# Half B's tap sums wait for half A's norm buffers; the second and third weights are split ahead of the second token block; edge factors are made later

## The chip, the core and the metric

The kernel runs on one core of a Trainium2 chip. TensorE (PE) multiplies matrices, VectorE (DVE), ScalarE (ACT) and GpSimd (POOL) work element by element, SyncE (SP) issues the DMA transfers, and each engine executes its own list of instructions strictly in the order in which it was built; semaphores hold an instruction until what it reads is there. The metric is the device time of one execution, in microseconds (us).

## What is computed

A decoder trunk of two layers over 2048 tokens of 1024 channels, in float32. In outline, with the parts that the change touches kept:

```python
h = rmsnorm(x, even_norm)
proj = h @ even_w_in                       # pool 512 | ssm 512 | gate 1024
u_pool, u_ssm, z = proj[..., :512], proj[..., 512:1024], proj[..., 1024:]
pooled = windowed_mean(u_pool, (2, 4, 8, 16)) - u_pool   # divided by min(pos, window)
y = concat(pooled @ pool_w * pool_scale, s5(u_ssm)) * silu(z)
x = x + y @ even_w_out

h = rmsnorm(x, odd_norm)
val, gt, z = split(h @ odd_w_in, 3)
c = causal_depthwise_conv(val * sigmoid(gt), conv_w) + conv_b      # 31 taps
c = layernorm(c) * ln_g + ln_b                                     # over the channels
x = x + (silu(c) * silu(z)) @ odd_w_out
out = rmsnorm(x, final_norm)
```

## The kernel before

The tokens are cut into two halves, A and B, of 1024 tokens, and each half into two blocks of 512. Every weight and every activation is split into a high part, rounded to the fast float32 format, and a low part, the rest; a product is three matmuls (high by high, high by low, low by high). ACT makes the high part and DVE the low one by a subtraction.

The PE's list is a row of units: for half A the layer-0 projections `A.s0` to `A.s3` (inputs of the state-space part), `A.pu`, `A.pz`, `A.z`, then the same for B; then `A.glu`, `A.o`, the layer-1 projections of A, `B.glu`, `B.o`, those of B, and at the end `A.q` and `B.q`, the two output projections. The first three units run block by block: `A.s0.0`, `A.s1.0`, `A.s2.0` on the first token block, then `A.s0.1` and so on. A unit's sums stand in one of three PSUM buffers `mm` until another engine has taken them out, so the fourth unit can't begin before the first is emptied. `B.q` ends with four units on B's second token block.

Nothing of the order is written out by hand. While the kernel is built, `Sched` runs all the work as threads (`gen`, `conv_load`, `ln_thread`, `x_rates` and others), each of which yields one operation at a time, or waits for a key (`Wait`, `done`), or for a free buffer (`Alloc`). From all threads' next operations it takes the one that can start first on its engine by its own clock; among those of one engine that could start within `SLACK` of it, the thread with the smallest priority number goes first. Its clock uses a duration for each operation (`tt`, `ts`, `mmb` and others) and adds a margin `PAD` after the producer. The chip sees only the lists that result: these numbers decide which instruction stands where, and no time in them is a time on the chip.

Four pieces of work matter below.

- **Weights.** `fetch_thread` loads them, `split_thread` makes the two parts. The first job has priority 0, the others have `RANK["split"]`, which is 2; the activations (`x_split`) have 1.
- **Token rates.** `x_rates` computes the reciprocal root mean square of each token: ACT squares, then for half A six small POOL instructions, a PE transposition of an 8 by 128 tile (`aux<-ident,sml`), an ACT copy, and a trip through the DRAM buffer `rsd` that spreads the rates over the partitions (`st<-rsd`). `post_u` needs them before it can empty a unit's `mm` (`po<-mm,st`).
- **State-space tables.** `ssm_tables` (DVE), `ssm_w` and `ssm_g` prepare four groups of tables, many small DMAs among them; `ssm_g` transposes a group's table in two lots on the PE (`aux<-ident,act`, four each) and ACT copies them out of the two `aux` buffers.
- **Tap sums and the norm.** `conv_thread` adds the 31 taps of a channel tile on DVE, in two accumulators from the pool `ca`, which has four tiles. Three of half B's eight channel tiles are summed on the PE instead (`pe_conv`). `ln_thread` normalizes one token block of one half over the channels: it loads four tiles, sums them, takes the mean with a PE product against `onesN` (`aux<-st,onesN`), squares on ACT, and applies the rate. Half A's two blocks (A0, A1) and B's second (B1) take their four tiles from `ca`, B's first (B0) from `act`; so A1 can load only when all four `ca` tiles are free. B0 and B1 start when half A's activations for `A.q` are all there.

`setup` makes `corr`, sixteen factors for each pooling window that correct the first tokens; `pool_thread` uses them.

Of the kernel before, what the change touches and what calls it, by code (L numbers as in the profile page):

```python
# [34 lines left out]
GATE_R = 'A.pz1'  # L35
GATE_S = 'B.s0.1'
SLACK = {"PE": 0.02, "V": 0.6, "A": 0.3, "G": 0.1, "SP": 0.3}
PAD = {("PE", True): 5.0, ("PE", False): 0.3, ("V", True): 1.0, ("V", False): 0.05, ("A", True): 1.0, ("A", False): 0.05}
SLOTS = dict(act=25, w=8, raw=2, st=8, po=2)
NSSM = 3  # L40
# [37 lines left out]
class Sched:  # L78
# [31 lines left out]
    def spawn(self, gen, prio, name=""):  # L110
        self.threads.append(Thread(gen, prio, name))
# [20 lines left out]
    def ready(self, op):  # L132
        r = 0.0
        for aps, wr in ((op.reads, False), (op.writes, True)):
            for ap in aps:
                nm, (lo, hi, p0, p1) = self.span(ap)
                dr = ap.space == bass.MemoryType.DRAM
                for (a, b, q0, q1), t, e, w in self.acc.get(nm, ()):
                    if dr and wr and w:
                        continue  # L140
                    if a < hi and lo < b and p0 < q1 and q0 < p1 and (wr or w) and not (e == op.eng == "PE"):
                        r = max(r, t + (PAD[op.eng, e == "SP"] if op.eng in "PE V A" else 0.05))
        return r

    def emit(self, op):
        start = max(self.clk[op.eng], op.ready)
# [102 lines left out]
def trunk(ctx, tc, io):  # L249
# [43 lines left out]
    def width(o):  # L293
        return int(np.prod(o.shape[1:]))
# [19 lines left out]

    def tt(o, a, b, op, eng=None):
        if eng is G:
            d = 1.0 + 0.2 * width(o) if op == ALU.pow else 0.6 + width(o) * 2e-3
            return Op("G", d, [a, b], [o], lambda: G.tensor_tensor(o, a, b, op))  # L318
        d = vdur(0.16, 1.035e-3, o, a, b)
        return Op("V", d, [a, b], [o], lambda: V.tensor_tensor(o, a, b, op))  # L320

    def ts(o, a, s1, s2=None, op0=ALU.mult, op1=None, eng=None):
        rd = [a] + [s for s in (s1, s2) if isinstance(s, bass.AP)]
        e = eng or V

        def emit():
            if op1 is None:
                e.tensor_scalar(o, a, s1, None, op0)  # L328
            else:
                e.tensor_scalar(o, a, s1, s2, op0, op1)  # L330
        if eng is G:
            return Op("G", 0.6 + width(o) * 1e-3, rd, [o], emit)
        return Op("V", 0.165 + width(o) * (1.03e-3 if isps(a) else 0.55e-3), rd, [o], emit)

    def stt(o, a, s, b, op0, op1):
# [171 lines left out]
    jobs = []  # L507
# [167 lines left out]
    def x_load(h, b, acts, gate=None, job=None):  # L675


        if gate:
            yield Wait(gate)
        if job:  # L680
            job.raw = yield Alloc("raw")
        for kp in range(4):
            yield from acts.alloc(kp, b)
            xt = yield Alloc("st")
            if job:
                r = jobs_parts[job][kp]
                yield dma(job.raw[:, r], job.src[:, r])
                done("raw", job, kp)
            yield dma(xt[:, :1024], io["xT"][h, b, kp])
            spawn(x_split(h, xt, acts, kp, b), 1, f"xs{h}{b}{kp}")  # L690
            done("x", h, b, kp)
# [787 lines left out]
    def conv_load():  # L1479
        for h, j in conv_order:  # L1480
            yield Wait(("g", h, j))
            gt = yield Alloc("cg")
            if h == 0:
                yield gset(gt[:, :HL], 0.0)
            else:
                yield dma(gt[:, :HL], gd[0][j][:, H - HL:H])
            yield dma(gt[:, HL:HL + H], gd[h][j])
            cgt[h, j] = gt
            yield Wait(("cw",))
            ca, cb = cas[h, j] = yield Alloc("ca", 2)  # L1490
            yield act(ca[:, :H], gt[:, 0:H], AF.Identity, bias=vc("conv_b", j), scale=cwt[:, j, 0:1])
            yield act(cb[:, :H], gt[:, 1:H + 1], AF.Copy, scale=cwt[:, j, 1:2])
            done("cg", h, j)
# [145 lines left out]
    def ln_thread(h, b, out, gate=None):  # L1639
# [5 lines left out]
        pool = "act" if h == 1 and b == 0 else "ca"  # L1645
        pools = (pool,) * 4
        ct = yield Alloc(pool, 4)
        cc = [c[:, :1024] for c in ct]
        for kp in range(4):
            yield dma(k2(cc[kp]), cd[h][kp][:, :, bs])  # L1650
# [197 lines left out]
    def setup():  # L1848
        yield act(junk[:, :16], mhalf, AF.Square)
        yield dma(vcol[:, :NV], io["vecs"])  # L1850
        done("vcol",)
        yield Wait(("x", 0, 1, 3))
        spawn(ssm_prep(), RANK["prep"], "prep")
        yield Wait(("boot", 3))
        for gi, w in enumerate(WINDOWS):
            yield ts(corr[:, gi, :], pos, float(w), 1.0 / w, ALU.min, ALU.mult)
        yield recip(corr, corr)
# [21 lines left out]
    jobs_parts[jobs[0]] = [slice(q * 256, q * 256 + 256) for q in range(4)]  # L1879
    spawn(main(), 4, "main")  # L1880
    spawn(setup(), 1, "setup")
    spawn(x_load(0, 0, h0[0], None, jobs[0]), 1, "x00")
    spawn(after(("x", 0, 0, 3), fetch_thread(jobs[1:])), 2, "fetch")
    spawn(split_thread(jobs[:1]), 0, "split0")
    spawn(after(("w", jobs[0]), split_thread(jobs[1:])), RANK["split"], "split")
    spawn(x_load(0, 1, h0[0], ("x", 0, 0, 3)), 2, "x01")
    spawn(x_rates(0, ("x", 0, 1, 3)), 3, "xr0")
    spawn(pool_fold(), 3, "fold")
# [73 lines left out]
```

## Time and profile before

| | |
|---|---|
| three runs | 1495.79, 1497.37, 1497.68 us; median 1497.37 |
| the profiled execution | 1496.72 us |
| its span, first to last instruction | 1494.9 us; 1.8 us lie around it |
| mean granted TensorE clock | 0.993 |
| busy: PE, DVE, ACT, POOL | 98%, 78%, 36%, 3% |

A row of the timeline gives start and duration in us, engine, line, operation, out<-in, shapes, how many, and in brackets the idle time of the engine before it with what ended it. A row of the waits gives engine, tile and line, what was waited for, and us in total, times, longest. A row of windows gives a stretch, the busy us of the engine asked for with its instructions, the granted TensorE clock, the share of DMA time and GB/s. A row of the chain gives start, us and what the end of the program hung on there.

### The profile page before, as it was taken

The page shows a single profiled execution, that of the slowest core. Times are in us where ns is not written, and L with a number is a line of the kernel's source. Part 1 is how long each engine was busy: PE and PEld are TensorE (multiplying, and loading weights), DVE is VectorE, ACT ScalarE, POOL GpSimd, SP SyncE. Part 2 cuts the span into 40 slices and gives each one's busy share as a digit, 9 for nine tenths or more (in the row PEclk, how much of TensorE's full clock was granted, in tenths as well). Part 3 has the DMA queues.
Part 4 walks back from the last instruction along what each step waited for, and adds up shares of the span by engine and source line. Part 5 has one row for each costly group of instructions (what it writes and reads, how often), then busy time and mean ns, then how long its engine had stood idle before and what let it go on. Part 6 is the DMA issues. An engine that isn't in the chain of part 4 may idle for free.

```text
span 1494.9 us, 17913 instructions
## 1 busy us (share of the span) xinstructions
PE 1460.0 (98%) x6672; PEld 1190.2 (80%) x6672; DVE 1159.5 (78%) x1435; ACT 545.2 (36%) x964; POOL 40.9 (3%) x103
## 2 busy tenths in 40 slices
PE   7898999999999999999999999999999999999997
PEld 5777888887788888888888888888888888878786
DVE  7987773999935124499999999996999997577852
ACT  6235331121143037212122431452235334446753
POOL 0100000000000001000000000100000000001000
PEclk9999999999999999999999999999999999999999
DMA  8579856677454456555655543646655468676853
GB/s 342 193 219 341 296 172 243 208 251 251 144 198 146 143 198 224 182 186 182 201 207 206 199 158 127 197 141 241 210 174 176 133 201 280 241 275 205 295 195 114
DMA packets 150311, 310.06 MB, mean 207 GB/s; under 512 B 38240, under 2 KB 60496, under 8 KB 150224
## 3 DMA queue, kind: packets, MB, share of 16 engines
q1 hardware_dynamic: 150224, 308.92, 60.7%
q8 instruction: 52, 0.85, 0.2%
q14 instruction: 35, 0.29, 0.1%
HBM read 192.18 MB, written 116.70 MB: 207 GB/s over the span
## 4 chain that ended last, share of the span: by engine, by line
PE 75%; DVE 11%; DMA 7%; SPq 2%; issue 2%; ACT 2%; POOL 0%; POOLq 0%; DVEq 0%; ACTq 0%
PE mm L402 70%; DVE st L320 4%; PE aux L402 3%; SPq L387 2%; DVE act L320 2%; DVE w L320 1%; DMA st<-x2d 1%; DVE st L348 1%; PE aux L416 1%; DMA y1d<-st 1%; DVE st L338 1%; DMA ca<-cd 1%; DMA st<-in_x 1%; DMA raw<-in_even_w_in 1%; DMA Md<-st 1%
## 5 line engine op out<-in xcount | busy, mean ns | idle before, releaser
L402 PE MATMUL mm<-act,w 128*128 128x512 f32 x4224 | 1002.6, 396 | 14.0 <-ACT act L364 6.4
L402 PEld LDWEIGHTS mm<-act,w 128*128 128x128 f32 x4224 | 792.1, 189 | 196.9 <-ACT act L364 6.9
L338 DVE SCALAR_TENSOR_TENSOR ca<-cg,cwt,ca 128x1024 f32<-128x1024 f32 (+1 forms) x435 | 463.3, 1136 | 4.3 <-ACT ca L364 4.3
L402 PE MATMUL mm<-w,act 128*128 128x512 f32 x1344 | 317.5, 396 | 1.1 <-DVE w L320 1.0
L402 PEld LDWEIGHTS mm<-w,act 128*128 128x128 f32 x1344 | 252.9, 189 | 60.3 <-DVE w L320 1.7
L320 DVE TENSOR_TENSOR w<-raw,w 128x1024 fp32r<-128x1024 f32 (+1 forms) x95 | 112.5, 1187 | 78.1 <-ACT w L352 76.6
L352 ACT CAST w<-raw 128x1024 fp32r<-128x1024 f32 (+1 forms) x95 | 96.6, 1017 | 118.9 <-PE mm L402 89.5
L364 ACT ACTIVATE junk<-st 128x1024 bf16<-128x1024 f32 (+1 forms) x64 | 54.0, 843 | 100.3 <-DVE st L320 81.2
L320 DVE TENSOR_TENSOR act<-st,act 128x512 fp32r<-128x512 f32 (+1 forms) x64 | 56.5, 922 | 25.9 <-ACT act L352 25.8
L364 ACT ACTIVATE po<-mm 128x1024 f32<-128x1024 f32 x28 | 28.8, 1028 | 126.0 <-PE mm L402 70.9
L364 ACT ACTIVATE st<-mm 128x1024 f32<-128x1024 f32 x24 | 24.7, 1027 | 130.6 <-PE mm L402 127.6
L352 ACT CAST act<-st 128x512 fp32r<-128x512 f32 (+1 forms) x64 | 52.0, 854 | 52.5 <-DVE st L338 15.6
L402 PE MATMUL aux<-st,act 128*128 128x64 f32 (+1 forms) x352 | 53.0, 293 | 1.4 <-DVE st L320 1.4
L320 DVE TENSOR_TENSOR st<-st,mm 128x512 f32<-128x512 f32 x48 | 31.0, 682 | 29.3 <-PE mm L402 29.0
L352 ACT COPY st<-aux 128x256 f32<-128x256 f32 (+3 forms) x46 | 18.0, 415 | 91.4 <-PE aux L402 78.6
L402 PEld LDWEIGHTS aux<-st,act 128*128 128x128 f32 x352 | 45.6, 191 | 6.0 <-DVE st L320 3.5
L318 POOL TENSOR_TENSOR sml<-sml,mhalf 128x1 f32<-128x1 f32 (+2 forms) x38 | 30.6, 817 | 650.4 <-DVE sml L328 355.4
L338 DVE SCALAR_TENSOR_TENSOR st<-st,mm 128x1024 f32<-128x1024 f32 x24 | 31.9, 1328 | 19.9 <-PE mm L402 13.1
L364 ACT ACTIVATE act<-act,mask 128x128 f32<-128x128 f32 x144 | 43.3, 390 | 8.7 <-DMA act<-band 8.7
L402 PE MATMUL mm<-act,act 128*128 128x512 f32 x192 | 45.1, 394 | 0.8 <-DVE st L320 0.8
L320 DVE TENSOR_TENSOR st<-st,act 128x512 f32<-128x512 f32 (+1 forms) x38 | 29.3, 772 | 20.9 <-DMA st<-x2d 14.9
L402 PEld LDWEIGHTS mm<-act,act 128*128 128x128 f32 x192 | 36.0, 188 | 9.5 <-DVE st L320 1.2
(148 smaller groups left out, 893.9 us busy)
## 6 DMA issues: line engine op xcount, KB each, us to landing
st<-x1d SPq DMA_DIRECT2D x48, 256.0 KB, 4.4
raw<-in_odd_w_in SPq DMA_DIRECT2D x24, 512.0 KB, 4.5
kept_h<-w SPq DMA_DIRECT2D x24, 512.0 KB, 3.0
kept_l<-w SPq DMA_DIRECT2D x24, 512.0 KB, 5.3
w<-kept_h SPq DMA_DIRECT2D x24, 512.0 KB, 3.7
w<-kept_l SPq DMA_DIRECT2D x24, 512.0 KB, 4.8
raw<-in_even_w_in SPq DMA_DIRECT2D x23, 512.0 KB, 5.4
st<-in_xT SPq DMA_DIRECT2D x16, 512.0 KB, 8.0
```

Of the source, the lines that this page charges most:

```text
L318: return Op("G", d, [a, b], [o], lambda: G.tensor_tensor(o, a, b, op))
L320: return Op("V", d, [a, b], [o], lambda: V.tensor_tensor(o, a, b, op))
L338: return Op("V", d, rd, [o], lambda: V.scalar_tensor_tensor(o, a, s, b, op0, op1))
L348: return Op("V", 0.2 + width(o) * 1.9e-3, rd, [o], lambda: V.tensor_tensor_scan(o, r.to_broadcast([128, width(o)]), x, ini, ALU.mult, ALU. ...
L352: return Op("A", adur(o, a, 0), [a], [o], lambda: A.copy(o, a))
L364: return Op("A", adur(o, a, n), rd, wr, lambda: A.activation(o, a, fn, **kw))
L387: lambda: SP.dma_start(out=o, in_=i))
L402: nc.tensor.matmul(o, w, x, start=s, stop=e)
L416: nc.tensor.transpose(o, a, idn)
```

## The change

Five edits. Half B's `conv_load` waits until A1 has its four `ca` tiles (`done("ln", h, b)` stands right behind that allocation). The second and third weights are split at priority 0, ahead of the activations of the second token block. The edge factors `corr` are made when `A.s3` begins, and not early in `setup`. The scheduler's margin for a PE operation that waits for a compute engine is 1.0 larger while its clock is below 200. Its durations for POOL operations are smaller. The last two change nothing but the order.

```diff
--- before.py
+++ after.py
@@ -35,6 +35,7 @@
 GATE_R = 'A.pz1'
 GATE_S = 'B.s0.1'
 SLACK = {"PE": 0.02, "V": 0.6, "A": 0.3, "G": 0.1, "SP": 0.3}
+EARLY, EARLY_END = 1.0, 200.0
 PAD = {("PE", True): 5.0, ("PE", False): 0.3, ("V", True): 1.0, ("V", False): 0.05, ("A", True): 1.0, ("A", False): 0.05}
 SLOTS = dict(act=25, w=8, raw=2, st=8, po=2)
 NSSM = 3
@@ -139,8 +140,15 @@
                     if dr and wr and w:
                         continue
                     if a < hi and lo < b and p0 < q1 and q0 < p1 and (wr or w) and not (e == op.eng == "PE"):
-                        r = max(r, t + (PAD[op.eng, e == "SP"] if op.eng in "PE V A" else 0.05))
+                        r = max(r, t + self.pad(op.eng, e == "SP", t))
         return r
+
+    def pad(self, eng, sp, t):
+
+        if eng not in "PE V A":
+            return 0.05
+        early = EARLY if t < EARLY_END and eng == "PE" and not sp else 0.0
+        return PAD[eng, sp] + early
 
     def emit(self, op):
         start = max(self.clk[op.eng], op.ready)
@@ -314,7 +322,7 @@
 
     def tt(o, a, b, op, eng=None):
         if eng is G:
-            d = 1.0 + 0.2 * width(o) if op == ALU.pow else 0.6 + width(o) * 2e-3
+            d = 0.35 + 0.2 * width(o) + 0.6 * (width(o) == 1) if op == ALU.pow else 0.19 + width(o) * 2e-3
             return Op("G", d, [a, b], [o], lambda: G.tensor_tensor(o, a, b, op))
         d = vdur(0.16, 1.035e-3, o, a, b)
         return Op("V", d, [a, b], [o], lambda: V.tensor_tensor(o, a, b, op))
@@ -329,7 +337,7 @@
             else:
                 e.tensor_scalar(o, a, s1, s2, op0, op1)
         if eng is G:
-            return Op("G", 0.6 + width(o) * 1e-3, rd, [o], emit)
+            return Op("G", 0.19 + width(o) * 1e-3, rd, [o], emit)
         return Op("V", 0.165 + width(o) * (1.03e-3 if isps(a) else 0.55e-3), rd, [o], emit)
 
     def stt(o, a, s, b, op0, op1):
@@ -1487,6 +1495,8 @@
             yield dma(gt[:, HL:HL + H], gd[h][j])
             cgt[h, j] = gt
             yield Wait(("cw",))
+            if h == 1:
+                yield Wait(("ln", 0, 1))
             ca, cb = cas[h, j] = yield Alloc("ca", 2)
             yield act(ca[:, :H], gt[:, 0:H], AF.Identity, bias=vc("conv_b", j), scale=cwt[:, j, 0:1])
             yield act(cb[:, :H], gt[:, 1:H + 1], AF.Copy, scale=cwt[:, j, 1:2])
@@ -1645,6 +1655,7 @@
         pool = "act" if h == 1 and b == 0 else "ca"
         pools = (pool,) * 4
         ct = yield Alloc(pool, 4)
+        done("ln", h, b)
         cc = [c[:, :1024] for c in ct]
         for kp in range(4):
             yield dma(k2(cc[kp]), cd[h][kp][:, :, bs])
@@ -1851,7 +1862,9 @@
         done("vcol",)
         yield Wait(("x", 0, 1, 3))
         spawn(ssm_prep(), RANK["prep"], "prep")
-        yield Wait(("boot", 3))
+
+    def pool_edges():
+        yield Wait(("u", "A.s3"))
         for gi, w in enumerate(WINDOWS):
             yield ts(corr[:, gi, :], pos, float(w), 1.0 / w, ALU.min, ALU.mult)
         yield recip(corr, corr)
@@ -1879,10 +1892,12 @@
     jobs_parts[jobs[0]] = [slice(q * 256, q * 256 + 256) for q in range(4)]
     spawn(main(), 4, "main")
     spawn(setup(), 1, "setup")
+    spawn(pool_edges(), 1, "edges")
     spawn(x_load(0, 0, h0[0], None, jobs[0]), 1, "x00")
     spawn(after(("x", 0, 0, 3), fetch_thread(jobs[1:])), 2, "fetch")
     spawn(split_thread(jobs[:1]), 0, "split0")
-    spawn(after(("w", jobs[0]), split_thread(jobs[1:])), RANK["split"], "split")
+    spawn(after(("w", jobs[0]), split_thread(jobs[1:3])), 0, "split1")
+    spawn(after(("w", jobs[2]), split_thread(jobs[3:])), RANK["split"], "split")
     spawn(x_load(0, 1, h0[0], ("x", 0, 0, 3)), 2, "x01")
     spawn(x_rates(0, ("x", 0, 1, 3)), 3, "xr0")
     spawn(pool_fold(), 3, "fold")
```

What stands elsewhere in the lists now, at three places.

**DVE in the first 20 us.** `act_18`, `act_22`, `act_25` are low parts of the activations (18 of the first token block, 22 and 25 of the second); `w_36<-raw_20,w_35` (before) and `w_35<-raw_20,w_34` (after) is the low part of the second weight. Before:

```order
L338 SCALAR_TENSOR_TENSOR act_18_350<-st_19_351,vcol,act_17_349 128x512
L344 RECIPROCAL corr<-corr 128x64
L338 SCALAR_TENSOR_TENSOR act_18_350<-st_19_351,vcol,act_17_349 128x512
L338 SCALAR_TENSOR_TENSOR act_22_356<-st_23_357,vcol,act_21_355 128x512 x2
L338 SCALAR_TENSOR_TENSOR act_25_363<-st_26_364,vcol,act_24_362 128x512 x2
L320 TENSOR_TENSOR w_36_402<-raw_20_354,w_35_401 128x1024
```

Of the change:

```order
L328 TENSOR_TENSOR w_35_398<-raw_20_354,w_34_397 128x1024
L346 SCALAR_TENSOR_TENSOR act_18_350<-st_19_351,vcol,act_17_349 128x512
L346 SCALAR_TENSOR_TENSOR act_22_356<-st_23_357,vcol,act_21_355 128x512
L346 SCALAR_TENSOR_TENSOR act_25_363<-st_26_364,vcol,act_24_362 128x512
L346 SCALAR_TENSOR_TENSOR act_22_356<-st_23_357,vcol,act_21_355 128x512
```

The low part of the second weight has moved ahead of five activation instructions and behind only one half of `act_18`; the `corr` instructions are gone from here.

**PE, the token rates and the state-space tables.** First the transposition of half A's token rates (`ident,sml`), among the matmuls of `A.s1.1` and `A.s2.1`. Before:

```order
L402 MATMUL mm_50_461<-act_32_386,w_35_401 128x512
L402 MATMUL mm_50_461<-act_31_385,w_36_402 128x512
L416 MATMUL aux_74_727<-ident,sml_37_404 8x128
L402 MATMUL mm_58_537<-act_21_355,w_48_459 128x512
L402 MATMUL mm_58_537<-act_22_356,w_48_459 128x512
```

Of the change:

```order
L410 MATMUL mm_50_455<-act_27_366,w_34_397 128x512
L410 MATMUL mm_50_455<-act_28_367,w_34_397 128x512
L410 MATMUL mm_50_455<-act_27_366,w_35_398 128x512
L424 MATMUL aux_68_667<-ident,sml_37_401 8x128
L410 MATMUL mm_50_455<-act_27_366,w_34_397 128x512
```

It stands nine matmuls of the projections, two products of `pool_fold` (`aux<-pwt,st`, eight instructions each on the chip) and a three-part transposition earlier. Then the second lots of the table transpositions, `act_140` and `act_160` (groups 1 and 2). Before:

```order
L402 MATMUL mm_166_1526<-act_21_355,w_146_1353 128x512
L416 MATMUL aux_175_1560<-ident,act_140_1330 128x128 x4
L402 MATMUL mm_166_1526<-act_11_339,w_145_1352 128x512
L402 MATMUL mm_166_1526<-act_24_362,w_145_1352 128x512
L402 MATMUL mm_166_1526<-act_12_340,w_145_1352 128x512
L402 MATMUL mm_166_1526<-act_25_363,w_145_1352 128x512
L402 MATMUL mm_166_1526<-act_11_339,w_146_1353 128x512
L402 MATMUL mm_166_1526<-act_24_362,w_146_1353 128x512
L416 MATMUL aux_177_1576<-ident,act_160_1450 128x128 x4
L416 MATMUL aux_178_1579<-ident,act_140_1330 128x128 x4
```

Of the change (`act_161` is group 2's table here):

```order
L410 MATMUL mm_176_1605<-act_14_344,w_152_1422 128x512
L410 MATMUL mm_176_1605<-act_27_366,w_152_1422 128x512
L424 MATMUL aux_188_1688<-ident,act_161_1481 128x128 x4
L410 MATMUL mm_176_1605<-act_17_349,w_151_1421 128x512
L410 MATMUL mm_176_1605<-act_31_382,w_151_1421 128x512
```

Group 2's second lot stands a unit and a half later among the projections, with 30 matmuls between its two lots, and group 1's are all ahead of it; group 3's two lots stand 18 and 24 matmuls later than they did.

**DVE, the norm of half A's second block.** `ca_885` and `ca_886` are the accumulators of half B's first channel tile before, `ca_926` and `ca_927` after; `ca_889` to `ca_892` are A1's four tiles. Before, half B's tap sums follow block A0's norm at once:

```order
L320 TENSOR_TENSOR st_883_7756<-st_883_7756,ca_858_7521 128x1024
L320 TENSOR_TENSOR st_884_7767<-st_884_7767,ca_859_7522 128x1024
L338 SCALAR_TENSOR_TENSOR ca_885_7788<-cg_869_7605,cwt,ca_885_7788 128x1024
L338 SCALAR_TENSOR_TENSOR ca_886_7789<-cg_869_7605,cwt,ca_886_7789 128x1024
L338 SCALAR_TENSOR_TENSOR ca_885_7788<-cg_869_7605,cwt,ca_885_7788 128x1024
```

Of the change, at the same place:

```order
L328 TENSOR_TENSOR st_884_7761<-st_884_7761,ca_859_7522 128x1024
L346 SCALAR_TENSOR_TENSOR st_886_7795<-st_886_7795,mm_885_7794 128x1024
L328 TENSOR_TENSOR st_893_7838<-ca_889_7818,ca_890_7819 128x1024
L328 TENSOR_TENSOR st_893_7838<-st_893_7838,ca_891_7820 128x1024
L328 TENSOR_TENSOR st_893_7838<-st_893_7838,ca_892_7821 128x1024
L328 TENSOR_TENSOR st_893_7838<-st_893_7838 128x512
```

A1's norm follows A0's, and the tap sums of half B come behind all of it. At the program's end that shows again. `mm_1183` and `mm_1193` are the third and the fourth of `B.q`'s eight units, the last two of B's first token block; `ca_1137` and `ca_1138` are the last two tiles of B1's norm and `act_1201`, `act_1206` the activations made of them:

```order
L328 TENSOR_TENSOR ca_1137_10151<-ca_1137_10151,st_1142_10181 128x1024
L328 TENSOR_TENSOR ca_1138_10152<-ca_1138_10152,st_1142_10181 128x1024
L346 SCALAR_TENSOR_TENSOR st_1184_10525<-st_1184_10525,sml_1196_10637,act_1103_9861 128x512
L346 SCALAR_TENSOR_TENSOR st_1185_10526<-st_1185_10526,sml_1197_10639,act_1103_9861 128x512
L328 TENSOR_TENSOR st_1198_10667<-st_1198_10667,ca_1137_10151 128x1024
L328 TENSOR_TENSOR st_1199_10675<-st_1199_10675,ca_1138_10152 128x1024
L328 TENSOR_TENSOR st_1194_10621<-st_1194_10621,mm_1193_10620 128x512
L328 TENSOR_TENSOR st_1195_10622<-st_1195_10622,mm_1193_10620 128x512
L328 TENSOR_TENSOR act_1201_10711<-st_1198_10667,act_1200_10710 128x1024
L328 TENSOR_TENSOR act_1206_10727<-st_1199_10675,act_1205_10726 128x1024
```

The last two activations of B's second block stand behind the instructions that take out the fourth unit; before, the last of them stood ahead of those of the third.

## The prediction

> **What bounds the kernel now.** I read the page first, then the waits of the PE, then its timeline where the waits lie.
>
> ```profile
> span 1494.9 us, 17913 instructions
> PE 1460.0 (98%) x6672; PEld 1190.2 (80%) x6672; DVE 1159.5 (78%) x1435; ACT 545.2 (36%) x964; POOL 40.9 (3%) x103
> ```
>
> The PE is busy for all but 34.9 us of the span. The start (raw data, first split) and the tail hold most of that, and no part of the change touches them; what can be won is the rest, and what slow clock costs behind a stall. These are the PE's waits in the first 200 us (engine, tile, line, what was waited for: us in total, times, longest):
>
> ```profile
> PE mm L402 <- ACT act L364: 6.4, 1, 6.4
> PE aux L416 <- ACT st L352: 4.9, 1, 4.9
> PE mm L402 <- DVE po L320: 3.9, 1, 3.9
> PE mm L402 <- DVE w L320: 2.6, 1, 2.6
> PE aux L416 <- DVE act L320: 1.1, 1, 1.1
> ```
>
> From 1240 us to the end the largest is this one:
>
> ```profile
> PE aux L402 <- DVE st L320: 1.8, 1, 1.8
> ```
>
> The 6.4 is the start. Four others before 200 us (12.5 us together) and the 1.8 lie where the change moves something. A stall costs more than its length, as the windows around three of them show (stretch, PE busy, instructions, granted clock, DMA share, GB/s):
>
> ```profile
> 50.00:60.00 10.00, 6.08 (x30) 0.83 0.62 225
> 140.00:150.00 10.00, 5.09 (x19) 0.70 0.99 398
> 1320.00:1330.00 10.00, 8.17 (x31) 0.92 0.79 293
> ```
>
> The profiled execution took 1496.72 us (span 1494.9 and 1.8 around it), 0.65 below the median of the runs. The sum is made against 1496.7.
>
> **Second and third weight.**
>
> ```profile
> 13.20 1.05 ACT L352 CAST w<-raw 128x1024 fp32r<-128x1024 f32 x1 [0.55 <-DMA raw<-in_even_w_in]
> ```
>
> That is the high part of the second weight; its low part, on DVE:
>
> ```profile
> 18.22 1.22 DVE L320 TENSOR_TENSOR w<-raw,w 128x1024 fp32r<-128x1024 f32 x1
> ```
>
> The high part is ready at 14.25, the low part at 19.44, since activations of the second block go first. Behind only one half of `act_18` it can end at 14.25 + 1.22 = 15.5. The second unit starts at about 16.6, so the 2.60 goes: −2.6 at best, 0 at worst (if the displaced activations of the first block hold the PE instead). One instruction of 1.22 us is put ahead of half of `act_18`, which may cost some tenths: **−2.5**. The activations of the second block are wanted only when `A.s0.1` begins, three units on.
>
> **The token rates.** The transposition, and the first evacuation that needs the rates:
>
> ```profile
> 45.16 0.27 PE L416 MATMUL aux<-ident,sml 128*8 128x128 f32 x1
> ...
> 53.80 3.90 DVE L320 TENSOR_TENSOR po<-mm,st 128x1024 f32<-128x1024 f32 x2 [0.66 <-DMA st<-rsd]
> ...
> 55.84 2.93 PE L402 MATMUL mm<-act,w 128*128 128x512 f32 x6 [3.92 <-DVE po L320]
> ```
>
> Beside it a long run of matmuls at full clock:
>
> ```profile
> 154.69 11.28 PE L402 MATMUL mm<-act,w 128*128 128x512 f32 x48
> ```
>
> The transposition at 45.16 starts the trip over `rsd`; the rates are back at 53.80, 8.6 us later, and the PE, with all three `mm` buffers full, waits 3.92. Its next six matmuls take 2.93; at 11.28/48 = 0.235 each they would take 1.41, so slow clock adds 1.5. The stall costs 5.4 in all, and that is the most to be won.
>
> Now the transposition stands earlier by nine matmuls (2.1 us), two fold products and a short transposition. One fold product in the chain, and the POOL instructions that make the input, with DVE's beside the last:
>
> ```profile
> 40.78 0.89 PE aux L402 x8
> ```
>
> ```profile
> 36.85 0.36 POOL L330 TENSOR_SCALAR sml<-sml 128x8 f32<-128x8 f32 x1 [33.52 <-ACT junk L364]
> ...
> 42.14 1.05 POOL L318 TENSOR_TENSOR sml<-sml,sml 128x8 f32<-128x8 f32 x1
> 42.09 1.03 DVE L320 TENSOR_TENSOR cg<-ca,pw 128x512 f32<-128x512 f32 x1
> ```
>
> So the place is 2.1 + 1.8 + 0.25, about 4 us, earlier, and the PE comes 2.5 us sooner besides: it is there at about 38.7. POOL ends at 43.2 now; the chain begins at 36.85 behind ACT's squares, which wait for loads and not for the PE. So a **new wait** stands here, of 4.5 us if the chain keeps its times, and of about 2.1 if it ends at 40.8 because its start moves forward with the split weights. I take 2.5 with 0.6 of slow clock, and set the old stall at nothing, since the trip then starts at about 41 instead of 45.2 and the PE has the same work to do meanwhile, less the nine matmuls that are behind the transposition now: 5.4 − 3.1 = **−2.3** (bounds −5.4 and +0.2: the wait at 4.5 and 1.1 of slow clock).
>
> On the clock: 3.92 of idling stands with 0.83 in the windows, 1.83 with 0.92. [...]
>
> The last POOL instruction runs beside a DVE instruction at 42.09. [...]
>
> **The state-space tables.** A load in the chain, then the PE's row where it waits and DVE's and the PE's for group 3:
>
> ```profile
> 133.61 8.42 DMA st<-in_x
> ```
>
> ```profile
> 145.93 1.97 PE L416 MATMUL aux<-ident,act 128*128 128x128 f32 x8 [4.91 <-ACT st L352]
> 147.55 7.27 PE L402 MATMUL mm<-act,w 128*128 128x512 f32 x24
> ...
> 164.15 0.69 DVE L320 TENSOR_TENSOR act<-cg 128x512 f32<-128x512 f32 x1
> 165.81 0.60 PE L416 MATMUL aux<-ident,act 128*128 128x128 f32 x4
> ```
>
> The 4.91: the second lot waits for `aux` buffers, which ACT empties, and ACT stands at its squares, which wait for a load of `in_x` (8.42 us on the chain). Now thirty matmuls (7 us) lie between the lots of group 2, so ACT's delay is covered. The stalls are 1.1 + 4.9; the 24 matmuls behind take 7.27 instead of 24 × 0.235 = 5.64 (1.6 more) and the eight transpositions 1.97 instead of twice 0.60 (0.8 more). So 8.4 could go.
>
> It doesn't all go, because group 3's last table is not made by the PE: DVE ends it at 164.84 and the PE takes it at 165.81. With everything gained up to here (2.5 + 2.3 + 8.4 = 13) the PE would come to its old place at 152.6; the new place is 18 to 24 matmuls, 4.2 to 5.6 us, later, so it is there at 157 to 158. If DVE's chain stayed at 164.8 the wait would be 7; the chain is ACT copies, SP issues, small DMAs and DVE in turn, and the ACT part behind the 8.42 load is not sped up, the part behind the PE is. Between a wait of 0 and of 7 (with 1.4 of slow clock) I take 4.4 and 1.0: 8.4 − 5.4 = **−3.0** (bounds −8.4 and 0).
>
> **The edge factors** are 0.40 and 0.54 us of DVE, among evacuations that the PE wants two units later: 0, at worst +0.9. **The `ca` order:** two ACT instructions per tile of `conv_load` wait; behind them in this thread stand only the taps, and other threads' work passes them: nothing on the PE by itself.
>
> **A1's norm.** The matmuls behind the stall of 1.83 in the chain, A0's last instructions on DVE, and the SP's rows for the norm's loads:
>
> ```profile
> 1328.79 9.78 PE mm L402 x36
> ```
>
> ```profile
> 1048.90 3.94 DVE L320 TENSOR_TENSOR st<-st,ca 128x1024 f32<-128x1024 f32 x3 [0.26 <-DMA st<-z1d]
> L387 SPq DMA_DIRECT2D ca<-cd x12: 518/610/1212, 1009.6 to 1317.6; - x12
> ```
>
> Of the twelve loads four are A0's (from 1009.6; A0 is done at 1052.8, 43 us later), four A1's (1251.6 in the trace) and four B1's (to 1317.6). A1's move to about 1053. Near 1328 the PE then no longer meets the mean product of B0 behind A1's work: the 1.83 goes, and 36 matmuls take 8.46 instead of 9.78 (1.3). Against it A1's own mean product now stands at about 1060, where nothing waited before, behind loads that follow A0's `z1d` and `y1d` traffic: 0 to 3.1; I take 2: 3.1 − 2 = **−1.1**. Half B's sums come 43 us later, and with them the norms of B0 and B1 come closer to the PE's need of them. For new waits there (mean products, last tiles) I take **+1.5**, between 0 and the 7 of the nearest long row (8.42 less what the PE has ahead).
>
> **Sum:** −2.5 − 2.3 − 3.0 − 1.1 + 1.5 = −7.4: 1489.3 for the profiled execution, 1490.0 at the median. The own range of this case: −3 (tables at 0, late waits at 3) to −13 (tables at −8.4, the rest as taken).
>
> **Rivals.**
>
> *The chains hold the PE at the same place.* The rates and group 3's tables are made by chains of loads, SP, ACT, DVE and POOL that don't get faster; then each gain turns into a wait at the next. The last wait on them is at 165.81: if group 3 is done at 164.8 as before, nothing won earlier lasts, and what stays is the norm's 1.1 and at most 1 of the rest: −2, 1495. For it speaks the pair 164.15/165.81, one us apart; against it that ACT's copies for the tables stood 5 us behind the PE's own stall.
>
> *B1's norm is late: slower.* It begins when the tap sums are out, and its four last tiles are wanted in the second lot of matmuls of the last block of `B.q`.
>
> ```profile
> 1250.00:1360.00 110.00, 76.55 (x84) 0.98 0.75 267
> ```
>
> That is DVE's window behind the sums. B1's last tile, and the start of the last block:
>
> ```profile
> 1433.59 1.22 DVE L320 TENSOR_TENSOR act<-st,act 128x1024 fp32r<-128x1024 f32 x1
> 1441.33 4.96 PE L402 MATMUL mm<-w,act 128*128 128x512 f32 x21
> ```
>
> The sums ended at 1250; now A1's norm has gone ahead of them, and in the 110 us behind 1250 its share of DVE's 76.6 us is replaced by sums of about the same length. So B1 starts between 1327 (no idling of DVE) and 1360 (idling as now). It ended at 1434.8 in the trace, 117 us after its last load; A0's took 43. The block begins at 1441.3 less the gains, at about 1434, and needs the last tiles some 9 us on, at 1443. From 1360 that is 83 us: it decides against the change if B1 takes longer. At 100 us the PE waits 16 with all else as forecast: 1506. For it: the 117, and that in the new order the last tiles of B1 stand behind evacuations of `B.q`. Against: the 117 held waits for nothing but DVE's turn, and 43 is half of what there is.
>
> *No new wait but the one on POOL.* Group 3 comes early with the rest, the norms meet the PE with time to spare: −2.5 − 2.3 − 8.4 − 3.1 = −16.3, 1481.
>
> **How the numbers follow.** The forecast (1490) 0.55; nothing won in the chains (1495) 0.17; B1 late (1500 and up, 1506 at its price) 0.10; nothing in the way (1481) 0.18. About 0.2%, 3 us, is what a measurement of this kernel can tell from no change: within it lie the second case and little of the first, above it the third. Faster 0.74, same 0.17, slower 0.09. The range goes from 1482, which takes in half of the best case, to 1497, which leaves the late norm out.
>
> **What the profile after would show.** Right: no PE wait on `w` near 16; the transposition of `sml` waits 2 to 4.5 us on POOL near 40, and no wait on `po` at 55 is left; near 146 no wait on ACT, but one of some us on DVE's `act` or its copies near 155 to 165; a product with `onesN` near 1060 that waits up to 3, and none of 1.8 near 1328; the last block of `B.q` begins without a wait, at about 1434. Wrong: a wait on `po` still there (the trip over `rsd` is late by itself), group 3 at 165 as before (the first rival), a wait on DVE of over 5 us behind 1430 (the second), or a new PE stall in 1050 to 1300, where the sums of half B now compete with evacuations.

## The result, and the profile after

The changed kernel takes 1488.62 us in the median (1486.76 to 1489.94, four runs) against 1496.58 before; the ratio is 0.9943, with a 95% interval of 0.9927 to 0.9959. Measured again in another group of runs it was 0.9948 (0.9936 to 0.9961). The forecast was 1490.0 in a range of 1482 to 1497. The profiled execution took 1489.94 us, 6.8 below the profiled one of before; the sum had been -7.4.

The page of the changed kernel, the rows that answer to those of before:

```profile
span 1488.2 us, 17921 instructions
...
PE 1459.1 (98%) x6672; PEld 1190.8 (80%) x6672; DVE 1159.7 (78%) x1435; ACT 544.9 (37%) x964; POOL 39.2 (3%) x103
```

The PE does the same 6672 instructions in nearly the same busy time (0.9 us less). Most of what the change won is idling: 5.8 of the 6.7 us of the span. The PE's waits of the changed kernel in the first 200 us, and then from 1240 us on:

```profile
PE mm L410 <- ACT act L372: 7.4, 1, 7.4
PE aux L424 <- DVE act L328: 5.9, 2, 5.3
PE mm L410 <- DVE act L346: 0.6, 1, 0.6
PE aux L424 <- POOL sml L326: 0.6, 1, 0.6
...
PE aux L410 <- DVE st L328: 2.5, 2, 1.5
PE mm L410 <- DVE st L328: 0.8, 1, 0.8
```

The waits on `w` (2.6) and on `po` (3.9) are gone, and so is the 1.8 at B0's mean product. The 4.9 on ACT is gone too, but a 5.3 on DVE at the same tables has come, and 2.5 at B1's products. The first row is the start, 1.0 us later here than in the profile of before; the second profile of the same kernel has 6.3 there, so it is no effect of the change.

The same places in the changed kernel's timeline of the PE:

```profile
39.30 0.27 PE L424 MATMUL aux<-ident,sml 128*8 128x128 f32 x1 [0.57 <-POOL sml L326]
...
160.28 1.09 PE L424 MATMUL aux<-ident,act 128*128 128x128 f32 x4 [5.34 <-DVE act L328]
161.02 4.57 PE L410 MATMUL mm<-act,w 128*128 128x512 f32 x12
...
1434.34 15.89 PE L410 MATMUL mm<-w,act 128*128 128x512 f32 x68
```

The rates' transposition stands at 39.30 and not at 45.16, the last block of `B.q` begins at 1434.34 and not at 1441.33, without a wait. Behind the 5.34 twelve matmuls take 4.57 instead of 12 × 0.235 = 2.82, and the four transpositions 1.09 instead of 0.60: 2.2 us of slow clock on top (the granted clock is 0.50 from 157.6 to 164.4).

Windows of the PE in the changed kernel:

```profile
50.00:60.00 10.00, 10.00 (x45) 1.00 0.96 331
140.00:150.00 10.00, 10.00 (x49) 1.00 1.03 412
150.00:160.00 10.00, 4.94 (x22) 0.88 0.98 364
160.00:170.00 10.00, 9.72 (x39) 0.78 0.90 263
1320.00:1330.00 10.00, 10.00 (x46) 1.00 0.51 184
```

The holes of 50 to 60, 140 to 150 and 1320 to 1330 are filled; the one of 140 to 150 has moved to 150 to 160.

To see where the time went I compare the start of the same instruction of the PE in two traces: the first matmul of a unit (the third unit; `A.z1`; a late state-space unit; a unit of half B's layer 1; the last block of `B.q`) and the end of the last matmul. The first line gives the times of before, the others the difference to it, in us, worked out from the PE's records. A row's own start (first column) varies by 1 us from execution to execution, and it is in all columns behind it. Further on two executions of the same lists differ by more: no_e and no_e_again, which are one kernel, stand 4.3 us apart at `A.z1`, and the change and after_again 1.3 us at 1015. So a difference of a few us between two rows can't be put down to an edit by the table alone.

| kernel | first matmul | third unit | A.z1 | state space | layer 1 | last block | end of PE |
|---|---|---|---|---|---|---|---|
| before | 6.4 | 26.5 | 190.2 | 435.4 | 1015.3 | 1441.3 | 1486.9 |
| the change | +1.0 | -2.4 | -7.6 | -7.2 | -5.7 | -7.0 | -6.8 |
| after_again | -0.1 | -3.0 | -8.5 | -7.8 | -7.0 | -9.1 | -8.9 |
| only_c | -0.2 | +0.6 | -1.1 | -1.1 | -0.6 | -4.4 | -2.7 |
| no_c | +0.1 | -2.7 | -8.1 | -7.2 | -6.0 | -0.9 | -0.9 |
| no_g | 0.0 | -2.2 | +1.5 | +1.6 | +2.4 | -1.1 | +0.6 |
| no_s | -0.1 | -4.0 | -8.9 | -8.4 | -6.4 | -7.0 | -6.8 |
| no_sk | -0.1 | +1.4 | -4.2 | -3.4 | -3.2 | -2.5 | -2.3 |
| no_e | -0.2 | -2.6 | -9.7 | -9.4 | -8.8 | -10.8 | -10.7 |
| no_e_again | +0.8 | -1.8 | -5.4 | -5.3 | -4.5 | -7.0 | -6.9 |
| no_se | 0.0 | -3.8 | -8.2 | -7.1 | -6.3 | -7.3 | -7.2 |
| g3_later | +0.5 | -2.4 | -6.3 | -6.3 | -5.1 | -3.8 | -3.6 |
| g4_both_later | -0.2 | -2.7 | -13.0 | -8.5 | -7.5 | -7.7 | -7.5 |
| c_and_g | +0.4 | +1.1 | -1.8 | -1.8 | -1.7 | -3.7 | -3.7 |

In both its profiles the change wins its 8 us ahead of 190, loses 1 to 2 up to 1015, and gets them back at the end.

### The profile page after: what moved, and what is told of

Its sections match the earlier page's. It is cut to its first block, busy times and chain, and to the rows that moved or that the text cites. A ratio compares the mean times of both kernels' runs of the same rounds, so it can differ in the third digit from the quotient of the medians.

```text
span 1488.2 us, 17921 instructions
## 1 busy us (share of the span) xinstructions
PE 1459.1 (98%) x6672; PEld 1190.8 (80%) x6672; DVE 1159.7 (78%) x1435; ACT 544.9 (37%) x964; POOL 39.2 (3%) x103
## 4 chain that ended last, share of the span: by engine, by line
PE 72%; DVE 13%; DMA 8%; ACT 3%; issue 2%; SPq 2%; POOL 0%; POOLq 0%; DVEq 0%; ACTq 0%
PE mm L410 68%; DVE st L328 4%; PE aux L410 3%; SPq L395 2%; DVE act L328 2%; DVE w L328 2%; DVE st L356 1%; DVE cg L328 1%; PE aux L424 1%; DMA st<-in_xT 1%; DMA x1d<-st 1%; DMA Gd<-st 1%; DMA raw<-in_odd_w_out 1%; DMA st<-x2d 1%; DVE st L346 1%
## 5 line engine op out<-in xcount | busy, mean ns | idle before, releaser
L328 DVE TENSOR_TENSOR st<-st,st 128x1024 f32<-128x1024 f32 (+1 forms) x36 | 35.3, 985 | 12.5 <-DMA st<-rsd 7.8
```

## The experiments

The letters: C is the wait of half B's tap sums for A1's norm buffers, S the split of weights two and three at priority 0, K the later edge factors, E the larger margin of the first 200 us, G the POOL durations. A name such as no_c is the change without C, only_c the kernel before with C alone. The measured ratios are against before, with their 95% intervals.

**Is the norm worth what its stall was?** only_c:

```diff
+            if h == 1:
+                yield Wait(("ln", 0, 1))
...
+        done("ln", h, b)
```

> The kernel before with one edit alone: half B's tap sums wait for A1's norm buffers. Nothing before 1000 us should differ. Theory (the PE's time is its idle time plus the slow clock behind it): the wait of 1.83 us near 1328 and the 1.3 us of slow matmuls behind it go, and B1's mean products, which the edit puts later, bring 2 to 2.5 us of new waits in place of 1.4 us of old ones in 1340 to 1410: -1.5 to -2.5 us against before, about 1494.5. Rival 1, the norm of B1 gets late: a wait of over 5 us behind 1430 and a time above before. Rival 2, the end of the program is set elsewhere: no change, 1496.6.

Measured: 0.9986 (0.9978 to 0.9995), 1495.55 us against 1497.65, 2.1 us less. The time is as expected, the way to it only in part. The 1.83 is gone, but the new waits of 2 to 2.5 at B1's products didn't come. A1's mean product waits 1.35 in its new place instead, and the PE's waits behind 1240 add up to 2.2 us against 3.9 before. The opposite experiment, no_c, takes the two lines of the wait out of the change:

> The changed kernel without the wait of half B's tap sums; all else of the change stays. Theory: the first 1000 us as in the changed kernel, then the stall of 1.8 us at B0's mean product comes back: 1.5 to 2.5 us over the changed kernel, about 1490.5. Rival, the norm is where most of the gain came from: 1494 or more.

Measured: 0.9998 (0.9989 to 1.0008), 1497.17 us. That is a miss by 7 us, and the most telling run of all: **the change without C gains nothing.** The time is the rival's, but not for its reason, since C alone is worth 2.1. Up to 1015 us it stands where the change does (-6.0 and -5.7 in the table); at the last block it has -0.9. The waits of the PE in no_c from 1240 us on:

```profile
PE aux L410 <- DVE st L328: 3.2, 2, 2.2
PE mm L410 <- DVE w L328: 3.1, 2, 2.4
PE aux L410 <- DVE st L336: 0.9, 1, 0.9
PE mm L410 <- DVE st L328: 0.8, 1, 0.8
```

Together 8.0, all on DVE, against 3.3 in the change and 3.9 before; behind the 2.4 the granted clock falls as well:

```profile
1390.00:1400.00 10.00, 7.62 (x27) 0.83 0.84 290
```

DVE's busy time behind 1250, first of no_c, then of the change, then the first two rows of before:

```profile
1250.00:1300.00 50.00, 33.95 (x38) 1.00 0.76 264
1300.00:1350.00 50.00, 39.69 (x48) 1.00 0.79 273
1350.00:1400.00 50.00, 42.06 (x56) 0.97 0.71 239
```

```profile
1250.00:1300.00 50.00, 47.89 (x62) 1.00 0.77 255
1300.00:1350.00 50.00, 47.66 (x63) 1.00 0.62 206
1350.00:1400.00 50.00, 38.94 (x50) 1.00 0.74 246
```

```profile
1250.00:1300.00 50.00, 33.76 (x39) 1.00 0.75 265
1300.00:1350.00 50.00, 35.34 (x37) 0.97 0.79 280
```

Without C DVE idles 26 us of the hundred behind 1250, because A1's, B0's and B1's norms stand there one behind the other and each begins with loads; the work it didn't do then it does behind 1350, where the PE wants weights and B1's products. With C, A1's norm lies at 1050 and sums fill the hundred. The idling alone isn't the cost: before idles 31 us of the same hundred, and its PE waits only 3.9. What no_c has besides is a PE that comes 6 us earlier. The loads follow the gain (no_c issues B1's at 1310.14, 5.4 us ahead of the 1315.57 of before), so the norms aren't late by themselves; what is late, as I read it, is the work that shares DVE with them. That the PE meets these waits is shown; that in another order of DVE's list they would be as long isn't, since the late lists of no_c and of before also differ in places.

**Which of the early edits brings the early gain?** no_g has the old durations of POOL back, two lines of numbers:

```diff
-            d = 0.35 + 0.2 * width(o) + 0.6 * (width(o) == 1) if op == ALU.pow else 0.19 + width(o) * 2e-3
+            d = 1.0 + 0.2 * width(o) if op == ALU.pow else 0.6 + width(o) * 2e-3
...
-            return Op("G", 0.19 + width(o) * 1e-3, rd, [o], emit)
+            return Op("G", 0.6 + width(o) * 1e-3, rd, [o], emit)
```

> The changed kernel with the old durations of the POOL operations in the scheduler: the transposition of the token rates then stands behind 144 matmuls of the projections and not 111 (120 in the kernel before), and group 3's tables behind 456 and 480 and not 540 and 552. Theory: the place of that transposition decides when the rates are back, so the wait on po near 50 to 60 us comes back, 33 matmuls (7.7 us) later than in the changed kernel, with 4 to 9 us of idling and 1.5 of slow clock; and the PE meets group 3's tables no later than in the kernel before: 1494 to 1500. Rival, the split weights alone bring the rates forward: within 1 us of the changed kernel, 1488 to 1490.

Measured: 0.9998 (0.9987 to 1.0009), 1497.28 us: as the theory had it in time, and the early gain is gone (+1.5 at `A.z1`). The wait is another than I named:

```profile
PE aux L410 <- DMA pwt<-in_pool_w: 4.9, 1, 4.9
PE aux L424 <- DVE act L328: 2.1, 1, 2.1
PE mm L410 <- DVE po L328: 1.9, 1, 1.9
PE aux L424 <- DVE st L328: 1.7, 1, 1.7
```

A fold product now waits for its own load near the place where the PE stood for `po`, and 1.9 on `po` stands behind it. These are numbers that only the scheduler uses and no engine executes, and without them the gain of the whole change is gone.

no_s puts the old split back, no_sk the old edge factors too:

```diff
-    spawn(after(("w", jobs[0]), split_thread(jobs[1:3])), 0, "split1")
-    spawn(after(("w", jobs[2]), split_thread(jobs[3:])), RANK["split"], "split")
+    spawn(after(("w", jobs[0]), split_thread(jobs[1:])), RANK["split"], "split")
```

> The changed kernel with the weights two and three split at the old priority. Theory: the wait of 2.6 us on w near 16 is back, the third unit begins 2 to 2.5 us later, and the token rates, 114 and not 111 matmuls in, make no new wait. Group 3's tables then stand 30 to 36 matmuls earlier in the row and the PE waits 5 to 9 us for them: 3 to 6 us over the changed kernel in the front, less at the end. Rival, the weights' wait only goes over into that of the rates: within 0.2% of the changed kernel, with a smaller wait on POOL near 40.

> The changed kernel with the old split and the edge factors made early again; left are the wait of the tap sums, the margin and the POOL durations. The low part of the second weight stands 22nd in DVE's list, as before. Theory: the two edits stand in for each other, and with neither the wait of 2.6 us on w near 16 is back; the token rates (102 matmuls in) then wait on POOL by 1 to 3 us; 2 to 4 us over the changed kernel, 1490 to 1493. Rival, neither has to do with the wait, and it is gone here too: 1489.

Measured: no_s 0.9951 (0.9939 to 0.9963), 1489.99 us; no_sk 0.9957 (0.9942 to 0.9972), 1490.52 us. In no_s no wait on `w` came back: the theory fell, and the time is that of its rival. The wait of 5.7 at group 3 is what the theory had named. The low part of the second weight in DVE's timeline of no_s:

```profile
13.83 1.22 DVE L328 TENSOR_TENSOR w<-raw,w 128x1024 fp32r<-128x1024 f32 x1
```

It stands at 13.83 without any priority, as early as in the change. In no_sk it is 22nd in DVE's list again, and the wait is back:

```profile
PE aux L424 <- DVE act L328: 4.0, 2, 3.6
PE mm L410 <- DVE w L328: 2.6, 1, 2.6
PE aux L424 <- POOL sml L326: 1.9, 1, 1.9
```

So with the edge factors moved away (K) the second weight comes early with S or without it; only with neither does the wait come back. Whether S alone would do it isn't shown: no run has S without K. The edge factors, which I had costed at nothing, held the second weight back by their place in the list (it starts 4.3 us later) and not by their 0.9 us. The time of no_sk stands within the interval of the change's. Its profile is 3 to 4 us behind the change's at `A.z1`, more than the wait, but that execution took 1494.42, the longest of its six, so the size is not to be relied on.

no_e has `EARLY = 0.0`; no_se has it with the old split besides; c_and_g is the kernel before with C and G alone:

> The changed kernel without the larger margin of the first 200 us. The rates stand at the same place (111), the lots of groups 0 to 2 are 12 to 18 matmuls later, group 3's at 540 and 546, half B's rates at 594. Theory: the margin isn't what brings the gain, the stall of 5.3 us at group 3 stays or shrinks by 1: within 2 us of the changed kernel. Rival, the margin is what keeps the PE off its producers: new waits of 2 us and more in 100 to 160, 1491 and above.

> The kernel without the larger margin once more, on the chip of this group. Theory: the margin costs the change 2 to 3 us: a ratio of 0.992 to 0.9935 to before. Rival, the lower time of no_e was chance: 0.9945 to 0.995, that of the changed kernel.

> The changed kernel without the split at priority 0 and without the larger margin; left are the wait of the tap sums, the later edge factors and the POOL durations. The low part of the second weight then stands 13th in DVE's list (12th in the changed kernel, 22nd before). Theory: moving the edge factors away is enough to clear the way for the second weight, and the margin is no gain: no wait on w near 16, and a time like that of no_e, 1485 to 1488. Rival, the split is needed: 2.6 us of waiting on w and 1490 or more.

> The kernel before with two edits, the wait of the tap sums and the POOL durations. The token rates are transposed 102 matmuls in, group 3's tables at 504 and 510. Theory: the wait on w (2.6) is as before, that on po near 56 (3.9 and 1.5 of slow clock) is gone since the rates come earlier by 18 matmuls, and the gain reaches the end since the tap sums wait: 4 to 6 us under before, 1492. Rival, the rates wait on POOL for as long as the PE waited for po: 1495, as with the wait of the tap sums alone.

Measured: no_e 0.9925 (0.9910 to 0.9941), 1485.69 us, and again 0.9934 (0.9919 to 0.9950), 1488.30 us; no_se 0.9945 (0.9930 to 0.9960), 1489.72 us; c_and_g 0.9964 (0.9952 to 0.9977), 1492.72 us. The margin brings nothing. The change without it was below the change both times (0.9925 beside the 0.9948 of after_again in the same group, and 0.9934 in another), but the intervals overlap, and no_se, without it too, stands with the change: whether the margin costs 1 or 2 us stays open. no_se has no wait on `w`, as the theory said, and 6.0 us at group 3, which it hadn't said. c_and_g hits in time: two of the five edits bring 4.6 us of the 8; the wait on `w` is there (2.6), the one on `po` is gone. But the rates wait 2.3 on POOL, and its profile shows only 1.8 us won at `A.z1`.

**Can the stall that is left be had?** g3_later holds group 3's lots back until `A.z0` begins:

```diff
+        if i == 3:
+            yield Wait(("u", "A.z0"))
         for a in range(2):
             gps = yield Alloc("aux")
```

> The changed kernel with one line more: the two lots of group 3's table transpositions wait until unit A.z0 begins, which puts them behind 576 and 588 matmuls and not 540 and 552. Theory: DVE's last table of group 3 was there at 160.1 us, the PE came 5.3 us too early and paid about 1.9 us of slow clock besides; 36 matmuls are 8.5 us, so both go: -6 to -7 us against the changed kernel, about 1482. Rival, the chain of ACT, SP and DVE behind the PE moves on with it, or another wait (the state-space part, the aux buffers) takes its place: 1487 to 1489.

Measured: 0.9964 (0.9950 to 0.9978), 1492.54 us, a miss. The lots no longer wait, but half B's rates, whose transposition had stood behind them, do, in the timeline of g3_later:

```profile
164.31 0.37 PE L424 MATMUL aux<-ident,sml 128*8 128x128 f32 x1 [6.33 <-DVE sml L328]
```

DVE makes group 3's tables and then those rates, in this order; the PE only meets the next of its results. So g4_both_later holds that transposition back too, by the same line ahead of it (`if h == 1`), and after_again goes with it for comparison:

> As g3_later, and the transposition of half B's token rates waits for unit A.z0 too (behind 576 matmuls and not 552), since the stall of 6.3 us was taken over by it: DVE had those rates at 164.2 us. From 410 us on the order is that of the changed kernel. Theory of the front: no wait over 1 us is left between 140 and 180, and A.z1 begins 6 to 8 us earlier than in the changed kernel. For the end two theories. One (waits add up): the whole 6 to 8 us arrive, about 1481. Other (from 627 us on DVE works without a pause on the tap sums, whose end doesn't depend on the PE, so what comes behind them comes when it does): the PE meets B's norms earlier by 7 us and waits there, the 2.5 us of waits near 1375 and 1406 grow by 3 to 7 us, and 0 to 4 us arrive: 1484 to 1488.

> The changed kernel once more, on the chip of the other three runs of this group, so that they can be compared with it directly: a ratio of 0.994 to 0.995 to before.

Measured: g4_both_later 0.9938 (0.9926 to 0.9950), 1488.64 us; after_again 0.9948, 1489.15 us: no difference that can be told. The front gains 4.5 us and not 6 to 8, since a wait of 2.2 is left at the rates: `A.z1` begins at -13.0 against -8.5. Then the PE meets this, in its timeline:

```profile
213.35 9.00 PE L410 MATMUL mm<-act,w 128*128 128x512 f32 x38 [2.74 <-DVE po L328]
```

Half B's activations come later with their rates, and DVE has them to do when the PE wants a unit emptied. That and longer waits in the state-space stretch leave 0.7 of 4.5 us at 435 (-8.5 against -7.8). The loss is long before the norms, so my second theory, that B's norms would take the gain, wasn't put to the test by it. no_e, whose gain at 1015 is the largest (-8.8), carries all of it to the end, and so does no_e_again (-4.5); that speaks against the theory as long as C is in.

## Why the prediction was right

The time was right, by luck in part: two of the sum's terms were off by some 2.5 us each in the profile of the change, in opposite directions, and an interaction that the sum didn't have made up for a loss that it didn't have either.

- **Second weight (-2.5).** Right in size: the 2.60 is gone and the low part starts at 13.85 instead of 18.22. Incomplete in cause: K without S does it as well (no_s, no_se), and with S besides it is worth no more; I had put K at 0.
- **Token rates (-2.3).** The mechanism was right, the size wrong: the new wait on POOL is 0.57, and 1.4 in the second profile, not 2.5, and no slow clock follows it (1.00 up to 157.6). Against the 5.4 of the old stall that is -4 to -4.8. The step that failed is the end of POOL's chain, put at 40.8 to 43.2: it ended at 39.25. Its start was earlier by only 0.8 us, its length was 3.2 and not 6.3, in this timeline of POOL in the changed kernel:

```profile
36.04 0.25 POOL L338 TENSOR_SCALAR sml<-sml 128x8 f32<-128x8 f32 x1 [32.70 <-ACT junk L372]
36.37 1.68 POOL L326 TENSOR_TENSOR sml<-sml,mhalf 128x8 f32<-128x8 f32 x1
...
39.03 0.22 POOL L326 TENSOR_TENSOR sml<-sml,sml 128x8 f32<-128x8 f32 x1
```

The 6.3 was that of one execution and no property of the order: only_c has the lists of before up to 1000 us, and there the chain takes 3.2 too (35.40 to 38.58; rows in the last section). It wins nothing there, since the transposition stands in its old place and the PE still waits 4.3 on `po`: it is the place that counts.

- **Tables (-3.0).** Too much: 5.34 and 0.59 of waits and 2.2 of slow clock make 8.1 against 8.4 before, so -0.3 (in the second profile the wait is 4.39, about 1 us less). The wait itself, put at 4.4, was near, though both its ends were earlier: the PE came at 154.9 and not at 157 to 158, and DVE was done at 160.1. The slow clock, put at 1.0, was twice that. The first rival is half right here: the tables' chain came 4.7 us earlier (159.44 + 0.69 = 160.13 on DVE against 164.84), the PE's gain was 7 to 8. Its "last wait" at 165.81 was none: in the kernel before the PE took that table without idling.

```profile
159.44 0.69 DVE L328 TENSOR_TENSOR act<-cg 128x512 f32<-128x512 f32 x1
```

- **Norm and late waits (-1.1 and +1.5).** In the table the stretch from 1015 to the end gives -1.1 and -1.9 where the sum had +0.4. The new waits of 2.5 came where they were expected, at B1's products; A1's mean product hardly waits in the change. As a size this is 2 us. As a reading it is the larger gap: I added C to the early edits as if each had its own worth. The runs with and without them are 1, 0.9986 (C alone), 0.9998 (the early edits alone) and 0.9943 to 0.9948 (both): apart they give 2.4 us, together 8. That they interact is shown by the times; why, only as far as the waits of no_c go.
- **What the sum lacked:** 1.5 to 2 us are lost between `A.z1` and 1015, some of it ahead of 435 and more behind, with about the idling that before has there. It is in most kernels of the table with an early gain; its cause stays open.
- **The rivals.** B1's norm wasn't late: the last block begins without a wait in the change. The best case failed at group 3.

## What to carry to other kernels

What is won early has to be followed to the end: look for the next stretch in which another engine is full or waits on loads, since an early gain can be worth nothing (0.9998) without an edit that is itself worth little (0.9986). In a list that a scheduler makes, an instruction's place can weigh more than its duration, so an edit that costs an engine 1 us and is "hidden" can still be what holds a later one back (0.9 us of edge factors put the second weight 4.3 us later here). And where a stall is moved off one result of an engine, ask for the same engine's next result: that is where the PE stood in g3_later, for 6.3 us. A chain that one profile shows can be twice as long as in another execution of the same lists (6.3 us in before, 3.2 in only_c), so a sum that rests on its end wants a second profile.

## What the runs showed of the hardware

Two things were not expected. First, four short POOL instructions that started 0.05 to 0.18 us after a DVE TENSOR_TENSOR with two operands in SBUF took 0.68 to 1.11 us and ended 0.05 to 0.07 us after it; in the changed kernel these forms take 0.20 to 0.25 us (38.40 to 39.25). In the kernel before, beside the pair at 42.09 and 42.14 that the prediction shows, POOL's row and DVE's a little earlier:

```profile
41.37 0.69 POOL L330 TENSOR_SCALAR sml<-sml 128x8 f32<-128x8 f32 x1
```

```profile
41.32 0.68 DVE L320 TENSOR_TENSOR act<-cg 128x512 f32<-128x512 f32 x1
```

POOL's 41.37 + 0.69 = 42.06 stands against DVE's 41.32 + 0.68 = 42.00, and 42.14 + 1.05 = 43.19 against 43.12. In no_sk it shows again, on a form that takes 0.22 and 0.25 us in the changed kernel (POOL's rows, then DVE's):

```profile
40.15 1.11 POOL L326 TENSOR_TENSOR sml<-sml,sml 128x8 f32<-128x8 f32 x1
...
41.62 0.68 POOL L326 TENSOR_TENSOR sml<-sml,sml 128x8 f32<-128x8 f32 x1
```

```profile
39.97 1.22 DVE L328 TENSOR_TENSOR w<-raw,w 128x1024 fp32r<-128x1024 f32 x1 [0.61 <-ACT w L360]
...
41.57 0.68 DVE L328 TENSOR_TENSOR act<-cg 128x512 f32<-128x512 f32 x1
```

41.26 against 41.19, and 42.30 against 42.25. Beside a DVE instruction that reads PSUM a POOL instruction was not longer: in before a TENSOR_TENSOR of 128x1 at 572.87 takes 0.54, beside two `act<-aux,vcol,act` that run from 572.07 to 573.48, and at 1483.38, with DVE idle, it takes 0.54 too. Two of this form take 1.91 at 586.15, beside a `w<-raw,w` that runs from 585.91 to 587.14, and 1.05 at 1477.26, with DVE idle. In the changed kernel no short instruction of the chain is held so. Nor is one in only_c, with the order of before, where DVE idled from 37.37 to 39.16. The last row of the chain there, and DVE's first after its idling:

```profile
38.38 0.20 POOL L326 TENSOR_TENSOR sml<-sml,sml 128x8 f32<-128x8 f32 x1
```

```profile
39.16 1.23 DVE L328 TENSOR_TENSOR w<-raw,w 128x1024 fp32r<-128x1024 f32 x1 [1.79 <-ACT w L360]
```

So, as I read these rows, whether POOL's chain takes 3.2 us or 5.5 to 6.3 (no_sk, c_and_g, before) hangs on how the two engines happen to meet. The change, after_again, no_s and no_g, all with K, have 3.2 to 3.3, and three of the four without it a long one, which is no proof that the order does it.

Second, the clock didn't follow a stall's length alone. A stall of 1.45 us in the changed kernel is followed by slow matmuls (0.84), one of 2.14 in after_again by none; the PE's windows, of the change and of after_again:

```profile
1400.00:1410.00 10.00, 8.55 (x36) 0.84 0.69 256
```

```profile
1370.00:1380.00 10.00, 7.86 (x33) 1.00 0.71 247
1380.00:1390.00 10.00, 10.00 (x45) 1.00 0.92 283
```

What its size was can be read from the traces of before and of the change. Up to the PE's end the clock in them is 1.00 or 0.50, and the stretches at 0.50 lie at stalls. In before they are 3.41 us at the stall of 3.92 (from 55.28), 6.83 at that of 4.91 (from 144.03) and 3.41 at that of 1.83 (from 1328.45); in the change 6.83 at that of 5.34 (from 157.59) and 3.41 at that of 1.45 (from 1406.87). The windows of the change show the last of them, and the stretch after it:

```profile
1406.87:1410.28 3.41, 3.41 (x9) 0.50 0.10 40
1410.30:1414.00 3.70, 3.70 (x17) 1.00 0.27 101
```

The 0.84 of ten us is thus 3.4 us at 0.50, worth 1.7 us. At group 3's tables of the change it is twice that, 157.6 to 164.4, of which 2.7 us pass while the PE still waits. The prediction had scaled slow clock with the stall's length; in these two traces it was 3.41 us behind 1.45, 1.83 and 3.92 alike, and none behind the 2.60 of before near 16 (1.00 up to 55.28). Which stalls set it off stays open.
